# A hybrid attention and state-space layer on one core: loads moved from SyncE's queue to GpSimd's, context products issued a quarter unit behind the latent ones, and one PSUM bank for the state updates of both directions

## The chip, the core and the metric

One core of a Trainium2 chip (trn2) runs the kernel as a single program. The engines are TensorE (PE; its weight loads are listed apart as PEld), VectorE (DVE), ScalarE (ACT), GpSimd (POOL) and SyncE (SP). DMAs can be issued from a queue of SP, ACT or POOL. The metric is the device time of one execution in microseconds (us); lower is better.

## The reference, cut to what matters

One layer (`D_MODEL` 2048) of a diffusion backbone for 512 latent tokens and 256 context tokens, in fp32. A vector `c` gives shift, scale and gate through `w_mod`; the tokens are RMS-normalised, modulated, and multiplied by one wide matrix `w_in`. Its columns feed two groups: windowed attention, and a bidirectional state-space scan (SSD) with four groups `g` of four heads. Both are gated, normalised and put through one output projection.

```python
shift, scale, gate = jnp.split((jax.nn.silu(c) @ w_mod + b_mod)[:, None, :], 3, axis=-1)
px = (rmsnorm(x, norm_g) * (1 + scale) + shift) @ w_in
pc = (rmsnorm(ctx, norm_g) * (1 + scale_c) + shift_c) @ w_in
...
a_cs = jnp.cumsum(a_t, axis=-1)
wts = cb[:, :, None] * jnp.exp(segsum(a_t))
y_diag = jnp.einsum('bgrcls,bcsgrp->bclgrp', wts, xdt)
states = jnp.einsum('bclgn,bgrcl,bclgrp->bcgrpn', bc, decay_states, xdt)
...
y_off = jnp.einsum('bclgn,bcgrpn,bgrcl->bclgrp', cc, prev, jnp.exp(a_cs))
...
x = x + gate * merge_groups(att_x, gx, y_x, zx, att_norm_g, ssd_norm_g, w_out)
```

The scan runs over chunks of 128 tokens, forwards and backwards; the latent scan starts from the state that the context tokens leave.

## The kernel before, in words

The program is written in one function, `emit`, with helpers. It goes through these stages: loading and normalising the latent tokens with the modulation (to some 140 us), the projections of values and step sizes (to 185 us), the SSD stage (unit 0 ends near 197 us; four groups to some 546 us), attention (to some 870 us), and the output projection.

**Units.** A unit is 128 columns of `w_in`. `load_unit` (L307 on) loads it in two halves `wr` of 512 KB from SP's queue, splits each quarter (four of the 16 K tiles of 128 rows) into a high part `wh` (ACT, L317) and a low part `wl` (DVE, by the helper at L55), and hands out (k, wh, wl) tile by tile. `proj` (L325 on) issues for each k three matmuls into `pj` (bank `a`, 128x512, latent tokens) and, for units that context tokens need, three into `pjc` (bank `b`, 128x256). All matmuls go through the helper at L49. The PSUM has eight banks, in pools "mm" (3), "sa" (2), "tp" (2), "pv" (1); `pj` and `pjc` come from "mm".

**A group of the SSD stage** (`ssd_group`, L485 on) has four units: two of `xs`, one of `bT`, each with context, and one of `cT` without. `conv_silu` (L470 on) runs the three-tap convolution of each: ACT at L476, DVE at L477 and L479, on the latent and the context half, then SiLU at L109 and L110; L479 is the last reader of the banks. Then come transposes, the states (`stc` from the context, `stx` in three steps per direction, each a matmul of 128x256 into a "tp" bank, and on DVE a product with the decay `etot` and an addition of the bank into `stt`), and for each of two pairs of heads: `z` (off-diagonal part), rows of running sums loaded from a DRAM scratch `csd` and spread over partitions (`ec`, two loads of 128 KB each, L570; `df`, 256 KB, L581), the decay matrices on ACT (L584 to L588) and DVE, and `yps`.

**Gate steps.** The modulation's gate (2048 columns) is summed on DVE: 64 steps `gate_step` (L280 on), called four times in each of units 1 to 16, each adding one 128x512 tile of `w_mod` times a scalar into `ga` (L299). The tiles `wg` are loaded two steps ahead into two buffers (L297); the tie `issue_after` puts each on SP's queue behind the unit's `wr` load. At each of four column blocks `ga` is cleared by a POOL memset (L289), gets its bias row (L291), and its sum over partitions is a matmul `gp`, stored to `grow`.

**What sets the order.** A planner orders each engine's instructions at build time, by their place in the source, by priorities (`tc.high_priority`: 200 for weights and the convolution, 150 for `df` and `ec` loads) and by costs of its own; it places an instruction where it expects its inputs to be there. It also puts in the waits. On the chip each engine and each DMA queue keeps that order: what waits at the head of a queue holds back what is behind it.

Of the kernel before, what the change touches and what calls it, by code (L numbers as in the profile page):

```python
# [14 lines left out]
P = 128  # L15
D = 2048
KT = 16
# [26 lines left out]
def emit(tc, xin, ctxT, wmod, wgate, bgate, wz, wvd, wu, wo, fng, vecs, cst, rope, out, dbg=None):  # L44
    nc = tc.nc
    es = ExitStack()

    def mm(o, l, r, start, stop):
        return nc.tensor.matmul(o, l, r, start=start, stop=stop)  # L49
# [13 lines left out]
    with es:  # L63
# [5 lines left out]
        def bank(tag, name, dt=F32, shape=(P, 512)):  # L69
            return ps.tile(list(shape), dt, tag=tag, name=name, bufs=pcount[tag])  # L70
# [23 lines left out]
        xl, cl = [], []  # L94
# [121 lines left out]
        for j in range(KT):  # L216
            mt = bank("pv", f"md_{j}", shape=(P, 260))
            md, ms = mt[:, 0:256], mt[:, 256:260]
            for hf in range(4):
                wm = su.tile([P, 4, 256], F32, tag="wm", name=f"wm_{j}_{hf}", bufs=7)  # L220
                nc.sync.dma_start(wm, wmod[j, :, hf * 4:hf * 4 + 4, :])
                for ki in range(4):
                    k = hf * 4 + ki
# [56 lines left out]
        def gate_step(ld):  # L280

            i = next(gsteps, None)
            if i is None:
                return
            n, k = divmod(i, KT)
            if k == 0:
                ga = wp.tile([P, 512], F32, tag="ga", name=f"ga_{n}", bufs=1)
                gacc.append(ga)
                nc.gpsimd.memset(ga, 0.0)  # L289
                with tc.issue_after(ld.ins):  # L290
                    nc.sync.dma_start(ga[0:1, :], bgate[:, n * 512:(n + 1) * 512])  # L291
            ga = gacc[n]
            for ii in range(len(gw), min(i + 2, 4 * KT)):
                n_, k_ = divmod(ii, KT)
                gw.append(gbuf(ii % 2, f"wg_{n_}_{k_}"))
                with tc.issue_after(ld.ins):
                    nc.sync.dma_start(gw[ii], wgate[n_, k_])  # L297
            wg = gw[i]
            geng.scalar_tensor_tensor(out=ga, in0=wg, scalar=sc0[:, k:k + 1], in1=ga, op0=ALU.mult, op1=ALU.add)  # L299
            if k == KT - 1:  # L300
                gp = bank("tp", f"gp_{n}", shape=(1, 512))
                mm(gp, ones[:, 0:1], ga, True, True)
                nc.scalar.activation(ga[0:1, :], gp, AF.Copy)
                nc.sync.dma_start(grow[:, n * 512:(n + 1) * 512], ga[0:1, :])
# [20 lines left out]
        def proj(u, with_ctx):  # L325
            a = bank("mm", f"pj_{u}")
            b = bank("mm", f"pjc_{u}", shape=(P, CT)) if with_ctx else None
            for k, wh, wl in load_unit(u):
                s0, s1 = k == 0, k == KT - 1
                mm(a, wh, xh[k], s0, False)  # L330
                mm(a, wh, xl[k], False, False)
                mm(a, wl, xh[k], False, s1)
                if with_ctx:
                    mm(b, wh, ch[k], s0, False)
                    mm(b, wh, cl[k], False, False)
                    mm(b, wl, ch[k], False, s1)
            return a, b


# [145 lines left out]
        def ssd_group(g, units):  # L485
# [41 lines left out]
            for d in range(2):  # L527
# [3 lines left out]
                mm(sp_, btok[:, 5, :], xw(d, 5), False, True)  # L531
                nc.scalar.activation(stt_[d][:, first, :], sp_, AF.Copy)
            for stp in range(3):
                for d in range(2):
                    c = stp if d == 0 else 3 - stp
                    nx = c + 1 if d == 0 else c - 1
                    sp_ = bank("tp", f"stx_{g}_{d}_{c}", shape=(P, 256))
                    mm(sp_, btok[:, c, :], xw(d, c), True, True)
                    tt(nc.vector, stt_[d][:, nx, :].rearrange("p (a b) -> p a b", a=4),
                       stt_[d][:, c, :].rearrange("p (a b) -> p a b", a=4),  # L540
                       etot[:, d, c, hs].unsqueeze(2).to_broadcast([P, 4, HD]), ALU.mult)
                    tt(nc.vector, stt_[d][:, nx, :], stt_[d][:, nx, :], sp_, ALU.add)
# [12 lines left out]
            for pr in range(2):  # L555
                tix = 2 * g + pr

                zs = []
                for d in range(2):
                    z = bank("sa", f"z_{tix}_{d}")  # L560
                    for c in range(NT):
                        cc = slice(c * P, (c + 1) * P)
                        mm(z[:, cc], stt_[d][:, c, pr * P:(pr + 1) * P], cT[:, cc], True, True)
                    zs.append(z)
                ecs = [w2(f"ec_{tix}_{d}", "ec", 3) for d in range(2)]

                for d in range(2):
                    with tc.high_priority(HB):
                        for hh in range(2):
                            nc.sync.dma_start(ecs[d][hh * 64:hh * 64 + 64], csd[d * 16 + tix * 2 + hh].partition_broadcast(64))  # L570
                    nc.scalar.activation(ecs[d], ecs[d], AF.Exp)
                yps = bank("pv", f"yps_{tix}")
                dm = []
                for hh in range(2):
                    r = tix * 2 + hh
                    dx = []
                    for d in range(2):

                        df = w2(f"df_{r}_{d}", "df", DF)
                        with tc.high_priority(HB):  # L580
                            nc.sync.dma_start(df, csd[d * 16 + r].partition_broadcast(P))  # L581
                        for c in range(NT):
                            cc = slice(c * P, (c + 1) * P)
                            nc.scalar.activation(df[:, cc], df[:, cc], AF.Relu, bias=cs[:, d, c, r:r + 1], scale=-1.0)  # L584
                        nc.scalar.activation(df, df, AF.Exp, scale=-1.0)
                        for c in range(NT):
                            cc = slice(c * P, (c + 1) * P)
                            nc.scalar.activation(df[:, cc], df[:, cc], AF.Copy, scale=dtt[:, d, c, r:r + 1])  # L588
                        tt(nc.vector, df, df, cb[d], ALU.mult)
                        dx.append(df)  # L590
                    tt(nc.vector, dx[0], dx[0], dx[1], ALU.add)
                    dm.append(dx[0])

                for c in range(NT):
                    cc = slice(c * P, (c + 1) * P)
                    for hh in (1, 0):
                        hl = pr * 2 + hh
                        mmo(yps[hh * 64:hh * 64 + 64, cc], xtok[:, c, hl * HD:hl * HD + HD], dm[hh][:, cc], True, True)
                for d in range(2):
                    tt(nc.vector, ecs[d], zs[d], ecs[d], ALU.mult)  # L600
                tt(nc.vector, ecs[0], ecs[0], ecs[1], ALU.add)
                yt = w2(f"yt_{tix}", "cve", 1)
                nc.vector.scalar_tensor_tensor(out=yt, in0=xs[pr][:, 0:S], scalar=dskh[:, tix:tix + 1], in1=yps,
                                               op0=ALU.mult, op1=ALU.add)
                tt(nc.vector, yt, yt, ecs[0], ALU.add)
                tt(nc.vector, yT[tix], yT[tix], yt, ALU.mult)
# [415 lines left out]
```

## Time and profile before

| | |
|---|---|
| median of three runs | 1055.41 us (1053.86 to 1055.51) |
| the profiled execution, its span | 1056.66 us, 1054.8 us |
| PE, PEld busy | 1011.6 us (96%), 818.4 us (78%) |
| DVE, ACT, POOL busy | 690.2 us (65%), 535.9 us (51%), 141.2 us (13%) |
| DMA | 147.29 MB in 53403 packets, 42.0% of 16 engines, all program loads on SP's queue |

Matmuls overlap: a 128x512 matmul shows 0.40 us, while the next begins 0.23 us later. So the busy share of PE says where it stands idle, and start-to-start times say what a product costs. "Idle before" of an engine is put down to what ended it. The granted clock of PE is 1.00 at its full 2.4 GHz and 0.5 at 1.2 GHz.

### The profile page before, as it was taken

Reading aid. Unit: us, or ns where it says so; the run is one execution under the profiler, and the core shown is the slowest. Engines: PE = TensorE matmul, PEld = TensorE weight load, DVE = VectorE, ACT = ScalarE, POOL = GpSimd, SP = SyncE. Lnnn points to the kernel's source line nnn. Section 1 sums busy time; section 2 is a strip of 40 time slices with the busy share of each in tenths; the row PEclk is TensorE's granted clock in tenths of the full one; section 3 lists DMA queues with packets and bytes.
Section 4 is the critical chain, followed back from the end, with each engine's and each line's share of the span. In section 5 each row is a group of like instructions: output and inputs, shape, how many; then the busy total and the mean of one; then the engine's idle time right before and its main releaser. Section 6 shows DMA issues by size and latency. Waiting matters only on the chain.

```text
span 1054.8 us, 15544 instructions
## 1 busy us (share of the span) xinstructions
PE 1011.6 (96%) x5682; PEld 818.4 (78%) x5682; DVE 690.2 (65%) x1346; ACT 535.9 (51%) x1236; POOL 141.2 (13%) x96
## 2 busy tenths in 40 slices
PE   5999999999999998999999999999999998999996
PEld 4676789887877887778787778777777777888885
DVE  4323378454875875785778888788797865333765
ACT  6222265247385384285364567576666654333333
POOL 0232300000000000000007000000000018644220
PEclk8999999999999999999999999999999998999999
DMA  9999963263273273264131311112111135442304
GB/s 332 382 340 351 340 219 120 92 214 121 78 232 122 80 219 113 89 203 127 61 106 61 100 41 61 41 40 81 40 58 59 45 135 195 141 167 90 106 27 159
DMA packets 53403, 147.29 MB, mean 140 GB/s; under 512 B 6056, under 2 KB 6568, under 8 KB 53072
## 3 DMA queue, kind: packets, MB, share of 16 engines
q1 hardware_dynamic: 53328, 146.31, 42.0%
q8 instruction: 44, 0.72, 0.3%
q14 instruction: 31, 0.25, 0.1%
HBM read 142.02 MB, written 4.27 MB: 139 GB/s over the span
## 4 chain that ended last, share of the span: by engine, by line
PE 58%; DVE 11%; DMA 9%; ACT 5%; issue 2%; POOL 1%; SPq 0%; ACTq 0%; DVEq 0%; POOLq 0%
PE pj L49 26%; PE o L49 14%; DMA wg<-in_wgate_dram 4%; PE pjc L49 4%; PE pv L49 3%; DMA ec<-csd 3%; PE ptp L768 3%; PE sl L49 3%; DVE df L55 2%; DVE wl L55 2%; PE sc L49 2%; DVE ga L299 1%; PE stx L49 1%; PE stc L49 1%; ACT df L588 1%
## 5 line engine op out<-in xcount | busy, mean ns | idle before, releaser
L49 PE MATMUL pj<-xh,wl 128*128 128x512 f32 x560 | 224.4, 401 | 1.5 <-DVE wl L55 1.4
L49 PE MATMUL pj<-xh,wh 128*128 128x512 f32 x560 | 225.8, 403 | 0.0
L49 PE MATMUL pj<-xl,wh 128*128 128x512 f32 x560 | 224.2, 400 | 0.0
L317 ACT ACTIVATE wh<-wr 128x512 fp32r<-128x512 f32 x140 | 87.6, 629 | 138.2 <-PE pjc L49 67.6
L55 DVE TENSOR_TENSOR wl<-wr,wh 128x512 fp32r<-128x512 f32 x140 | 100.1, 718 | 62.7 <-ACT wh L317 55.3
L49 PEld LDWEIGHTS pj<-xh,wl 128*128 128x128 f32 x560 | 105.8, 189 | 22.8 <-DVE wl L55 2.4
L49 PEld LDWEIGHTS pj<-xh,wh 128*128 128x128 f32 x560 | 106.2, 190 | 16.8 <-ACT wh L317 3.5
L49 PEld LDWEIGHTS pj<-xl,wh 128*128 128x128 f32 x560 | 106.3, 190 | 13.4
L55 DVE TENSOR_TENSOR wol<-wo,woh 128x512 fp32r<-128x512 f32 x56 | 54.4, 985 | 65.2 <-ACT woh L858 58.9
L49 PE MATMUL pjc<-chq,wh 128*128 128x256 f32 x224 | 66.5, 297 | 11.3 <-DVE xs L479 11.3
L858 ACT ACTIVATE woh<-wo 128x512 fp32r<-128x512 f32 x56 | 34.8, 629 | 73.4 <-PE o L49 65.3
L299 DVE SCALAR_TENSOR_TENSOR ga<-wg,sc,ga 128x512 f32<-128x512 f32 x64 | 47.9, 748 | 34.4 <-DMA wg<-in_wgate_dram 34.4
L49 PE MATMUL pjc<-clq,wh 128*128 128x256 f32 x224 | 65.6, 293 | 0.0
L49 PE MATMUL pjc<-chq,wl 128*128 128x256 f32 x224 | 63.8, 285 | 0.0
L49 PEld LDWEIGHTS pjc<-chq,wh 128*128 128x128 f32 x224 | 42.9, 191 | 22.3 <-ACT wh L317 14.2
L55 POOL TENSOR_TENSOR hacc<-hacc,hsq 128x512 f32<-128x512 f32 x14 | 20.4, 1457 | 290.0 <-ACT hsq L666 286.6
L772 ACT ACTIVATE ph<-ptp 128x512 fp32r<-128x512 f32 x72 | 41.1, 597 | 28.2 <-PE ptp L768 26.7
L49 PE MATMUL o<-woh,hsh 128*128 128x512 f32 x128 | 52.0, 407 | 3.1 <-ACT part L877 3.1
L55 DVE TENSOR_TENSOR pl<-ptp,ph 128x512 fp32r<-128x512 f32 x72 | 48.5, 684 | 7.9 <-ACT ph L772 7.7
L743 ACT ACTIVATE pe<-sl,nm 128x256 f32<-128x256 f32 (+1 forms) x64 | 33.6, 525 | 35.7 <-DVE nm L741 34.0
L49 PE MATMUL o<-wol,hsh 128*128 128x512 f32 x128 | 51.2, 400 | 0.0
L49 PE MATMUL o<-woh,hsl 128*128 128x512 f32 x128 | 51.1, 399 | 0.0
(282 smaller groups left out, 2294.0 us busy)
## 6 DMA issues: line engine op xcount, KB each, us to landing
wr<-in_wu_dram SPq DMA_DIRECT2D x70, 512.0 KB, 3.7
wm<-in_wmod_dram SPq DMA_DIRECT2D x64, 512.0 KB, 8.7
wg<-in_wgate_dram SPq DMA_DIRECT2D x64, 256.0 KB, 3.4
wo<-in_wo_dram SPq DMA_DIRECT2D x32, 512.0 KB, 3.9
df<-csd SPq DMA_DIRECT2D x32, 256.0 KB, 3.9
wsr<-in_wz_dram SPq DMA_DIRECT2D x16, 448.0 KB, 5.9
wr_v<-in_wvd_dram SPq DMA_DIRECT2D x16, 288.0 KB, 3.4
xt<-in_xin_dram SPq DMA_DIRECT2D x8, 512.0 KB, 4.7
```

Of the source, the lines that this page charges most:

```text
L49: return nc.tensor.matmul(o, l, r, start=start, stop=stop)
L55: eng.tensor_tensor(out=o, in0=a, in1=b, op=op)
L299: geng.scalar_tensor_tensor(out=ga, in0=wg, scalar=sc0[:, k:k + 1], in1=ga, op0=ALU.mult, op1=ALU.add)
L317: nc.scalar.activation(wh, rr, AF.Copy)
L588: nc.scalar.activation(df[:, cc], df[:, cc], AF.Copy, scale=dtt[:, d, c, r:r + 1])
L743: nc.scalar.activation(pe[:, 0:nl * P], sl, AF.Exp, bias=nm[:, i:i + 1], accum_out=sm[:, i, 0:1])
L768: nc.tensor.transpose(tp[:, i * P:(i + 1) * P], pt[i][:, n * P:(n + 1) * P], ident)
L772: nc.scalar.activation(ph, tp, AF.Copy)
L858: nc.scalar.activation(wh, wr[:, i, :], AF.Copy)
```

## The change

It has three parts. Gate weights `wg`, and the rows of running sums `ec` and `df`, are issued from POOL's queue instead of SP's, the gate weights without the tie to the `wr` load. In `proj` the context products of four K tiles are issued together after the latent products of these four. In the state updates both directions of a step write two halves of one "tp" bank instead of a bank each. Nothing else is changed, and the same sums are computed.

```diff
@@ gate_step
             for ii in range(len(gw), min(i + 2, 4 * KT)):
                 n_, k_ = divmod(ii, KT)
                 gw.append(gbuf(ii % 2, f"wg_{n_}_{k_}"))
-                with tc.issue_after(ld.ins):
-                    nc.sync.dma_start(gw[ii], wgate[n_, k_])
+                nc.gpsimd.dma_start(gw[ii], wgate[n_, k_])
@@ proj
             b = bank("mm", f"pjc_{u}", shape=(P, CT)) if with_ctx else None
+            late = []
             for k, wh, wl in load_unit(u):
                 s0, s1 = k == 0, k == KT - 1
                 mm(a, wh, xh[k], s0, False)
                 mm(a, wh, xl[k], False, False)
                 mm(a, wl, xh[k], False, s1)
                 if with_ctx:
-                    mm(b, wh, ch[k], s0, False)
-                    mm(b, wh, cl[k], False, False)
-                    mm(b, wl, ch[k], False, s1)
+                    late.append((k, wh, wl))
+                    if k % 4 == 3:
+                        for kk, h, l in late:
+                            mm(b, h, ch[kk], kk == 0, False)
+                            mm(b, h, cl[kk], False, False)
+                            mm(b, l, ch[kk], False, kk == KT - 1)
+                        late = []
@@ ssd_group
             for stp in range(3):
+                sp2 = bank("tp", f"stx_{g}_{stp}", shape=(P, 2, 256))
                 for d in range(2):
                     c = stp if d == 0 else 3 - stp
                     nx = c + 1 if d == 0 else c - 1
-                    sp_ = bank("tp", f"stx_{g}_{d}_{c}", shape=(P, 256))
+                    sp_ = sp2[:, d, :]
                     mm(sp_, btok[:, c, :], xw(d, c), True, True)
...
-                            nc.sync.dma_start(ecs[d][hh * 64:hh * 64 + 64], csd[d * 16 + tix * 2 + hh].partition_broadcast(64))
+                            nc.gpsimd.dma_start(ecs[d][hh * 64:hh * 64 + 64], csd[d * 16 + tix * 2 + hh].partition_broadcast(64))
...
-                            nc.sync.dma_start(df, csd[d * 16 + r].partition_broadcast(P))
+                            nc.gpsimd.dma_start(df, csd[d * 16 + r].partition_broadcast(P))
```

## Rows read from the trace of the kernel before

**Rows 1.** Busy time by stretch, the SSD stage: start:end, length, then busy us (instructions) by engine.
```profile
197.00:546.00 349.00, 333.74 (x1911) 279.80 (x1910) 237.25 (x419) 190.33 (x456) 1.58 (x3) 0.99 0.45 137
```
**Rows 2.** Waits of PE: engine, line, what for; total us, times, longest.
```profile
PE pjc L49 <- DVE xs L479: 11.3, 7, 3.2
```
**Rows 3.** Timeline of PE: start us, us, instruction, and idle time before it.
```profile
394.97 0.28 PE L49 MATMUL pjc<-chq,wh 128*128 128x256 f32 x1
...
395.33 0.39 PE L49 MATMUL pj<-xh,wh 128*128 128x512 f32 x1
...
397.89 0.40 PE L49 MATMUL pj<-xh,wl 128*128 128x512 f32 x1
401.52 0.35 PE L49 MATMUL pjc<-chq,wh 128*128 128x256 f32 x1 [3.24 <-DVE xs L479]
...
319.73 0.36 PE L49 MATMUL pjc<-chq,wh 128*128 128x256 f32 x1 [0.74 <-DVE xs L479]
...
380.70 0.36 PE L49 MATMUL pjc<-chq,wh 128*128 128x256 f32 x1 [0.84 <-DVE xs L479]
```
**Rows 4.** Busy time by stretch, 2 us each; the granted clock stands after POOL's count.
```profile
240.00:242.00 2.00, 2.00 (x16) 1.88 (x15) 1.36 (x2) 2.00 (x6) 0.00 (x0) 1.00 0.14 37
...
402.00:404.00 2.00, 2.00 (x11) 2.00 (x11) 1.99 (x3) 1.48 (x4) 0.00 (x0) 0.51 0.18 53
404.00:406.00 2.00, 2.00 (x8) 1.66 (x8) 1.36 (x2) 1.94 (x5) 0.00 (x0) 0.64 0.92 303
```
**Rows 5.** Timeline of DVE ahead of the wait at 401.52.
```profile
397.23 0.75 DVE L299 SCALAR_TENSOR_TENSOR ga<-wg,sc,ga 128x512 f32<-128x512 f32 x1 [3.19 <-DMA wg<-in_wgate_dram]
...
400.25 0.47 DVE L477 SCALAR_TENSOR_TENSOR xs<-pjc,v_sb,xs 128x255 f32<-128x255 f32 x1
400.64 0.74 DVE L479 SCALAR_TENSOR_TENSOR xs<-pj,v_sb,xs 128x511 f32<-128x511 f32 x1
```
**Rows 6.** Waits of DVE and ACT from 197 to 560 us.
```profile
DVE ga L299 <- DMA wg<-in_wgate_dram: 31.9, 24, 3.2
...
ACT df L584 <- DMA df<-csd: 15.0, 13, 3.4
...
ACT ec L571 <- DMA ec<-csd: 9.6, 7, 2.6
```
**Rows 7.** Waits of SP's queue from 197 to 560 us.
```profile
SPq L312 <- DVE wl L55: 121.6, 31, 10.1
SPq L297 <- DVE ga L299: 64.1, 43, 7.0
```
**Rows 8.** Timeline of SP's queue, two loads in a row.
```profile
392.21 0.33 SPq L297 DMA_DIRECT2D wg<-in_wgate_dram  x1
392.58 0.45 SPq L570 DMA_DIRECT2D ec<-csd  x1
```
**Rows 9.** Loads: count, KB, median us to landing; issue ns min/median/max, first and last start.
```profile
wg<-in_wgate_dram SPq DMA_DIRECT2D x64, 256.0 KB, 3.4
...
df<-csd SPq DMA_DIRECT2D x32, 256.0 KB, 3.9
...
ec<-csd SPq DMA_DIRECT2D x32, 128.0 KB, 5.6
...
L297 SPq DMA_DIRECT2D wg<-in_wgate_dram x64: 327/328/710, 157.1 to 485.5; - x64
```
**Rows 10.** POOL: a group of the page (busy us, mean ns, idle before), and its timeline.
```profile
L55 POOL TENSOR_TENSOR hacc<-hacc,hsq 128x512 f32<-128x512 f32 x14 | 20.4, 1457 | 290.0 <-ACT hsq L666 286.6
...
265.20 0.53 POOL L289 MEMSET ga<- 128x512 f32 x1 [127.75 <-DMA grow<-ga]
```
**Rows 11.** Timeline of SP's queue, the next two gate loads.
```profile
271.30 1.43 SPq L297 DMA_DIRECT2D wg<-in_wgate_dram  x2
```
**Rows 12.** State updates: matmul (ns min/median/max, first and last start), and two additions on DVE's timeline.
```profile
L49 PE MATMUL stx<-xw,btok x48: 377/379/483, 273.4 to 522.4; 128*128 128x256 f32 x48
...
274.38 0.94 DVE L55 TENSOR_TENSOR stt<-stt,stx 128x256 f32<-128x256 f32 x2
```

## The prediction, made before the changed kernel was run

> **What bounds it now.** I read first the busy time by stretches, then who waits for whom on TensorE (PE), then single boundaries in the timeline. The change touches only the SSD stage, 197 to 546 us: there PE is busy for 333.74 of 349 us [rows 1], so without new idle time elsewhere all that can be won is some 15 us of idle time and what a lowered clock costs. Of that idle time 11.3 us stand in seven waits of one kind: the first context product `pjc` of a projection unit waits for VectorE's (DVE's) L479 of the unit before [rows 2]. The reason is the PSUM pool: three "mm" banks, so the new `pjc` gets the bank of the old `pj`, and that is free when the convolution has read it.
>
> The reader should look at one such place [rows 3]. The new unit's `pj` begins at 395.33 and twelve of its products are issued up to 397.89; then PE stands for 3.24 us until L479 is done. So the planner already puts twelve latent products ahead of the first context product, and they don't suffice. The waits at 319.73 (0.74) and 380.70 (0.84) are the shortest of the seven; the other five are 1.57 us or more each. The 3.24 us cost more than themselves: behind them the granted clock is 0.51 and 0.64 for 2 us each, between the levels of 1.2 and 2.4 GHz [rows 4], which loses 2 x 0.49 + 2 x 0.36 = 1.7 us.
>
> Why is L479 late? On DVE a gate step waits 3.19 us for its weights, and the convolution is behind it [rows 5]. Over the stage DVE waits 31.9 us in 24 places for gate weights, and ScalarE (ACT) 15.0 and 9.6 us for the rows of running sums `df` and `ec` [rows 6]. The loads themselves wait at the head of SyncE's (SP's) one queue: 64.1 us for a gate buffer that DVE still reads, 121.6 us for a `wr` buffer [rows 7]. At 392.21 a gate load goes out, and the `ec` load behind it only at 392.58 [rows 8].
>
> **The context products.** Number and length stay. In the interleaved order three context products take 395.33 - 394.97 = 0.36 us, so 0.12 each [rows 3]. The last latent product of a unit is followed by three of them before and by twelve after, so `pj` is whole 9 x 0.12 = 1.08 us earlier against the unit's end, and the planner, which knows this, can put the convolution of `pj` that much further ahead of gate steps and `df` work on DVE and ACT. Each of the seven waits can shrink by that, but not below nothing: 5 x 1.08 + 0.74 + 0.84 = 7.0 us. With 3.24 cut to 2.2 I expect no fall of the clock behind it, as it stays at 1.00 behind the wait of the same kind that ends at 239.7 [rows 4]: 1.7 us more. Bounds: nothing, if the backlog and not the end of `pj` sets the convolution's start; and 8.9 us, if L479 of `pj` also overtakes the `pjc` half of L477 that now stands between (0.39 us from 400.25 to 400.64 [rows 5], 5 x 1.47 + 1.58). The `wh` and `wl` buffers stay in use to the end of the same quarter, so nothing new waits there.
>
> **The other queue.** SP loses 64 gate loads at 0.33 us of issue and 32 each of `df` and `ec` [rows 9]; it keeps the `wr` loads, and since no row of the stage has ACT waiting for `wr`, that alone is worth nothing. GpSimd (POOL) gets all 128. They still stand in one queue: a gate load that waits for DVE holds the `df` and `ec` behind it as before; only the waits for `wr` are taken out. Three memsets of `ga` are in that queue too; the first runs at 265.20 [rows 10] and the next gate load went out at 271.30 [rows 11], so it holds nothing back. The trace has no load issued from POOL. From below: no dearer than SP's 0.33 us. From above: POOL's two-input work on 128x512, 1.46 us; its memset of the same tile takes 0.53 [rows 10]. I take 0.53, as writing without reading is nearest to issuing, so 0.2 us more per load. Gate loads take 3.4 us to land [rows 9], and two buffers make the steps wait for them, so each of the 24 waits grows by 0.2: 4.8 us on DVE. About half of this reaches PE, as much of DVE's waiting falls where PE has work: +2.4 us. Against that stands that the `wr` waits no longer hold up loads; rows 7 show them, but not a load that was late by them, so I count nothing. The Trainium skill (DMA: Bandwidth & Descriptors, section "Latency and other measured facts") gives some 1 us to the first byte from GpSimd's queue against 0.6 us from SP's; no run here shows it. By that the term would be about 4.8 us instead of 2.4, an estimate.
>
> **The state updates.** Three steps in four groups take one bank instead of two. The matmul is 0.38 us, and the two additions now run as a pair, 0.94 us from 274.38 [rows 12]. No wait of PE or DVE for them is in the rows, so nothing is to be won; they lie between `pj` products. Taken at 0; the bounds stand with the rival below.
>
> **The sum.** The profiled execution took 1056.66 us (its span 1054.8 and 1.86 around it), 1.25 over the median of the runs. 1056.66 - 7.0 - 1.7 + 2.4 = 1050.4, so 1049.1 against the median of 1055.41. A measurement here can tell some 0.2% (2 us) from no change.
>
> **Rivals.**
> - **POOL issues dearly (slower).** At 1.46 us each of the 24 waits grows by 1.13: 27.1 us on DVE, half of it on PE 13.6. Less 8.7 from the context products that is +4.9: 1060.3; if all of it got through, 1073.8. It turns slower where 12 x (price - 0.33) passes 8.7, so at 1.05 us per load. For it: 128 loads in one in-order queue, in bursts of four `ec`. Against: POOL is idle in this stage but for memsets. 0.27.
> - **The deferral does nothing.** The planner already has twelve products ahead of the wait, and if DVE's backlog sets L479, the order that is written out changes nothing: 1055.4 + 2.4 = 1057.8. 0.15, half of it within 0.2%.
> - **The shared bank makes PE wait.** If the second direction's matmul may not write the bank while DVE adds the first, each of twelve pairs is a round trip: one addition (0.42) and a handover (L479's end at 401.38 to 401.52, 0.14), 0.56 x 12 = 6.7 us at worst, if PE stands meanwhile: 1049.1 + 6.7 = 1055.8. The rows speak half against it: other products lie between, which the planner can use. 0.07. The Trainium skill (PSUM — Partial Sum Buffer, section "PSUM bank collisions raise a hardware error") states that two engines must not touch one bank at once even at different addresses, so such a wait has to be there; no row here has such a pair.
> - **The planner sorts it all out.** With other costs for POOL's loads it may put gate steps where their data is there, and the convolutions first: then all of the 11.3 and the clock's 1.7 go, 13.0 us: 1042.4. For it: real loads came later than the order of DVE's steps assumed, 24 times. 0.15.
>
> **How the numbers follow.** My forecast, 1049.1, has 0.36. Faster is that and the last rival, 0.51; slower the first rival and half of the second, 0.34; within 0.2% the other half and the shared bank, 0.15. The forecast's own range is 1044 to 1055 (8.9 won and no dearer queue, or nothing but the clock's 1.7). Since both signs hold much, the range goes down to 1040 for the last rival and up to 1064, past 1060.3 part of the way to 1073.8.
>
> **What would show it.** Right: the seven waits of `pjc` for `xs` L479 sum to 3 to 5 us; runs of twelve `pjc` all through a unit; on DVE both halves of the `pj` convolution adjacent; no 0.5 clock near 403; waits for gate weights around 37 us. Wrong: these waits at 11 us or more (the queue, if gate waits grew with them; the backlog, if they didn't); new waits of PE's `stx` for DVE's `stt` (the bank); `ec` or `df` landing over 2 us later than 5.6 and 3.9 (POOL's issue). If gate waits shrink well under 30 us, the planner has moved the steps.

## The result, and the profile after

The kernel after takes 1064.63 us (median of 4 executions, 1063.37 to 1065.74) against 1054.89 us for the kernel before in the same sessions (1053.86 to 1055.51). The ratio is 1.0109, with a 95% interval of 1.0081 to 1.0138; the two medians alone make 1.0092, 9.7 us. The profiled execution of after took 1063.37 us, its span 1061.5. So the change costs some 10 to 11 us, where a gain to 1049.1 was forecast. The time lies inside the range, and on the other side of the sign.

Busy time by stretch of after: start:end, length, busy us (instructions) of PE, PEld, DVE, ACT and POOL, granted clock, DMA share, GB/s. The first row answers to [rows 1], the other three are three groups of the SSD stage.
```profile
197.00:546.00 349.00, 330.28 (x1880) 276.83 (x1879) 234.63 (x414) 185.46 (x447) 69.19 (x129) 0.99 0.45 135
262.00:345.00 83.00, 76.92 (x441) 64.27 (x440) 56.96 (x98) 45.70 (x111) 17.17 (x32) 0.98 0.48 140
345.00:427.00 82.00, 77.81 (x446) 65.34 (x444) 56.50 (x98) 45.26 (x110) 17.69 (x33) 0.98 0.47 140
427.00:507.00 80.00, 74.20 (x431) 62.81 (x431) 55.30 (x97) 44.62 (x109) 16.62 (x31) 0.98 0.46 133
```
The same view of before, for the two stretches where its clock was below 1.00:
```profile
190.00:262.00 72.00, 68.42 (x363) 58.24 (x361) 39.11 (x72) 35.73 (x80) 0.00 (x0) 0.98 0.49 150
...
345.00:427.00 82.00, 77.69 (x444) 65.08 (x443) 56.94 (x98) 45.79 (x111) 0.53 (x1) 0.98 0.47 141
```
In the same 349 us PE is busy 3.5 us less, so idle time grew. The clock lost about 245 x 0.02 = 4.9 us in after, 154 x 0.02 = 3.1 us in before (rounded to 0.01, so to some 2 us).

Who waits for whom in after, 197 to 560 us: engine, line, what for; total us, times, longest. These answer to [rows 2, 6].
```profile
PE pjc L49 <- DVE xs L484: 9.3, 4, 3.1
PE pjc L49 <- ACT wh L316: 7.2, 3, 3.0
PE yps L49 <- DVE df L55: 3.5, 2, 2.7
...
DVE ga L298 <- DMA wg<-in_wgate_dram: 33.3, 29, 3.7
...
ACT df L590 <- DMA df<-csd: 17.5, 13, 3.0
ACT ec L577 <- DMA ec<-csd: 9.7, 6, 3.2
...
POOL wg L296 <- DVE ga L298: 88.6, 47, 5.9
```
(Lines have moved: the convolution is L482 and L484, the gate step L298, its load L296, the split of the weights on ACT L316.) The waits of `pjc` are 16.5 us instead of 11.3, and 7.2 of them are new: they wait for ACT, not for the convolution. Two places show how. First the timeline of PE and of DVE at the worst of the four:
```profile
318.99 0.35 PE L49 MATMUL pjc<-chq,wh 128*128 128x256 f32 x1 [3.14 <-DVE xs L484]
...
320.62 0.41 PE L49 MATMUL pjc<-chq,wl 128*128 128x256 f32 x1
320.83 0.63 PE L49 MATMUL pj<-xh,wh 128*128 128x512 f32 x1
```
```profile
314.96 0.74 DVE L482 SCALAR_TENSOR_TENSOR xs<-pj,v_sb,xs 128x511 f32<-128x511 f32 x1
317.43 0.75 DVE L298 SCALAR_TENSOR_TENSOR ga<-wg,sc,ga 128x512 f32<-128x512 f32 x1 [1.73 <-DMA wg<-in_wgate_dram]
318.10 0.74 DVE L484 SCALAR_TENSOR_TENSOR xs<-pj,v_sb,xs 128x511 f32<-128x511 f32 x1
```
The planner did bring the convolution of `pj` forward, but put a gate step between its two halves, and that waits for its load. PE stands for 3.14 us, and then a product of 0.40 us takes 0.63: the clock is down, its granted share being 0.51 from 320 to 322 us. The waits at 403.56 and 488.30, of 2.1 and 2.8 us, are the same place in the next two groups. Then the timeline of ACT and PE:
```profile
291.99 0.63 ACT L577 ACTIVATE ec<-ec 128x512 f32<-128x512 f32 x1 [2.31 <-DMA ec<-csd]
...
295.98 0.62 ACT L316 ACTIVATE wh<-wr 128x512 fp32r<-128x512 f32 x1
```
```profile
296.65 0.36 PE L49 MATMUL pjc<-chq,wh 128*128 128x256 f32 x1 [2.17 <-ACT wh L316]
```
A row that lands late holds ACT, and the next quarter's `wh` behind it is late for PE. This too comes again in the next two groups.

The loads of after (count, KB, median us to landing; then the gate load's issue in ns, min/median/max) answer to [rows 9]:
```profile
wg<-in_wgate_dram POOLq DMA_DIRECT2D x64, 256.0 KB, 3.5
df<-csd POOLq DMA_DIRECT2D x32, 256.0 KB, 4.1
ec<-csd POOLq DMA_DIRECT2D x32, 128.0 KB, 5.1
...
L296 POOL DMA_DIRECT2D wg<-in_wgate_dram x64: 538/538/715, 137.1 to 490.5; - x64
```
Nothing in them is far from before: an issue of 0.54 us, landings within 0.5 us of [rows 9]. What cost 10 to 11 us had to be found by parts.

### The profile page after: what moved, and what is told of

The parts are those of the page before. It is cut to its first block, busy times and chain, and to the rows that moved or that the text cites. A ratio compares the mean times of both kernels' runs of the same rounds, so it can differ in the third digit from the quotient of the medians.

```text
span 1061.5 us, 15568 instructions
## 1 busy us (share of the span) xinstructions
PE 1012.6 (95%) x5682; PEld 819.3 (77%) x5682; DVE 692.1 (65%) x1346; ACT 536.5 (51%) x1236; POOL 209.5 (20%) x224
## 4 chain that ended last, share of the span: by engine, by line
PE 73%; DMA 8%; DVE 6%; ACT 6%; issue 4%; POOL 2%; SPq 0%; ACTq 0%; POOLq 0%; DVEq 0%
PE pj L49 25%; PE o L49 14%; PE zps L49 7%; DMA wg<-in_wgate_dram 5%; PE vps L49 4%; PE md L49 3%; PE pv L49 3%; PE pjc L49 3%; PE ptp L774 3%; PE sl L49 3%; DMA ec<-csd 2%; PE sc L49 2%; PE stx L49 1%; DVE df L55 1%; ACT df L594 1%
## 5 line engine op out<-in xcount | busy, mean ns | idle before, releaser
L316 ACT ACTIVATE wh<-wr 128x512 fp32r<-128x512 f32 x140 | 87.6, 628 | 140.2 <-PE pjc L49 68.9
L49 PE MATMUL pjc<-chq,wh 128*128 128x256 f32 x224 | 65.0, 290 | 16.5 <-DVE xs L484 9.3
L298 DVE SCALAR_TENSOR_TENSOR ga<-wg,sc,ga 128x512 f32<-128x512 f32 x64 | 47.9, 748 | 33.3 <-DMA wg<-in_wgate_dram 33.3
L296 POOL DMA_DIRECT2D wg<-in_wgate_dram x64 | 35.0, 547 | 171.8 <-DVE ga L298 88.6
L55 POOL TENSOR_TENSOR wsl<-wsr,wsh 128x896 fp32r<-128x896 f32 x16 | 33.9, 2118 | 101.4 <-ACT wsh L231 101.4
```

The lines of the kernel that those rows point to most:

```text
L55: eng.tensor_tensor(out=o, in0=a, in1=b, op=op)
L296: nc.gpsimd.dma_start(gw[ii], wgate[n_, k_])
L316: nc.scalar.activation(wh, rr, AF.Copy)
```

## The experiments

All times below are medians beside runs of before on the same chip; ratios are to before with their 95% interval. "Stage" is the time from the first product into `cst_ps` to the first of the last `yps`, read from PE's timeline of the one profiled execution (before 215.72 to 544.52, after 212.99 to 550.47). "`pjc` waits" is all that PE waits before `pjc` products there. The table names each kernel by its text of expectation. That execution need not be the median one: before's took 1056.66 us, and those of `wa` and `ra`, 1069.41 and 1081.1, are 5 us over their medians. So differences of stages hold to some 5 us.

| kernel | gate loads, rows, weights on | us | ratio | stage us | `pjc` waits us |
|---|---|---|---|---|---|
| before | SP, SP, SP | 1052 to 1055 | 1 | 328.8 | 11.3 |
| after | POOL, POOL, SP | 1064.63 | 1.0109 (1.0081 to 1.0138) | 337.5 | 16.5 |
| `a_only`: deferral alone | SP, SP, SP | 1047.65 | 0.9962 (0.994 to 0.9983) | 321.5 | 5.3 |
| `c_only`: shared bank alone | SP, SP, SP | 1048.28 | 0.9951 (0.9928 to 0.9973) | 324.4 | 10.6 |
| `ac`: both | SP, SP, SP | 1047.21 | 0.9953 (0.9932 to 0.9974) | 321.4 | 5.4 |
| `st`: no tie | SP, SP, SP | 1048.32 | 0.9972 (0.9951 to 0.9993) | 322.6 | 8.3 |
| `b_only`: queue alone | POOL, POOL, SP | 1076.32 | 1.0223 (1.0181 to 1.0264) | 351.4 | 23.5 |
| `bw` | POOL, SP, SP | 1064.58 | 1.0102 (1.0066 to 1.0139) | 340.3 | 19.4 |
| `br` | SP, POOL, SP | 1071.13 | 1.0169 (1.0132 to 1.0205) | 346.0 | 22.6 |
| `pool_stage` | POOL, POOL, POOL | 1061.23 | 1.0094 (1.0064 to 1.0124) | 333.6 | 15.8 |
| `full_stage`: after, so | POOL, POOL, POOL | 1056.71 | 1.0052 (1.003 to 1.0074) | 329.9 | 10.1 |
| `wa` | SP, SP, ACT | 1064.44 | 1.0108 (1.0066 to 1.0151) | 346.1 | 23.9 |
| `ra` | SP, ACT, SP | 1076.02 | 1.0227 (1.0172 to 1.0281) | 350.0 | 25.5 |

**1. Which of the three parts?** Each part alone, and the deferral with the bank. `a_only` has the hunk of `proj` alone, `c_only` that of the state updates, `b_only` the three hunks with `nc.gpsimd`, `ac` the first two of these:
```diff
 # b_only
-                with tc.issue_after(ld.ins):
-                    nc.sync.dma_start(gw[ii], wgate[n_, k_])
+                nc.gpsimd.dma_start(gw[ii], wgate[n_, k_])
...
-                            nc.sync.dma_start(df, csd[d * 16 + r].partition_broadcast(P))
+                            nc.gpsimd.dma_start(df, csd[d * 16 + r].partition_broadcast(P))
```
Expected, for the deferral alone:

> Only the context products are deferred; the loads stay on SyncE's queue and the state updates keep a bank each. Theory Q (the queue: loads issued from GpSimd's queue make the gate and row waits longer, and the loss of 9.7 us is theirs): this kernel gains what the prediction gave it, 1045 to 1051 us. Theory D (the deferral: the planner now takes the convolution apart, with gate steps and their waits between its two halves, and the bank comes free later): this kernel carries the loss, 1060 to 1066 us. Theory S (the shared bank): within 2 us of before.

For the queue alone:

> Only the loads of gate weights and of the rows of running sums go to GpSimd's queue. Theory Q: 1060 to 1068 us, with the waits of VectorE for gate weights and of ScalarE for rows longer than before (31.9, and 15.0 and 9.6 us). Theory D: within 3 us of before, 1052 to 1058 us. Theory S: within 2 us of before.

For the bank alone:

> Only the state updates of both directions share a bank. Theory S: 1058 us or more, with new waits of TensorE or VectorE in the state updates. Theories Q and D: within 3 us of before.

For the deferral and the bank:

> Context products deferred and the shared bank, loads left on SyncE's queue: the change without its queue part. Theory Q: 1045 to 1052 us. Theory D: 1060 to 1066 us, as the changed kernel. If the parts act on one another through the order that the planner makes, it lies neither at the sum of the two kernels with one part each nor at one of these values.

Measured: the queue alone costs 2.2%, some 23 us, more than the 1060 to 1068 us expected; deferral, bank and both together each gain 0.4 to 0.5%, and for the bank nothing was expected. So the loss is the queue's, all of it. With deferral and bank it costs 1.0109 - 0.9953 = 1.6%, some 16 us. The two profiled spans say where: after 1061.5, `ac` 1045.5, 16.0 us apart. PE's waits at `pjc` and `yps` are 20.0 us in after and 5.4 + 3.2 = 8.6 in `ac`, 11.4 more; the clock, 1.00 in every stretch of `ac`, lost 4.9 us in after: 16.3 together. PE's waits with `a_only`, then `ac`, as in [rows 2]:
```profile
PE pjc L49 <- DVE xs L484: 5.3, 6, 1.2
```
```profile
PE pjc L49 <- DVE xs L484: 5.4, 6, 1.2
```
What a long wait costs beyond itself shows in `b_only`, PE's timeline:
```profile
326.25 0.36 PE L49 MATMUL pjc<-chq,wh 128*128 128x256 f32 x1 [4.21 <-DVE xs L478]
...
326.96 0.41 PE L49 MATMUL pjc<-clq,wh 128*128 128x256 f32 x1
327.17 0.41 PE L49 MATMUL pjc<-chq,wl 128*128 128x256 f32 x1
```
Products that begin 0.12 us apart at full clock begin 0.21 apart here, and the granted clock is 0.50 from 328 to 330 us. In `b_only` the clock was 0.95, 0.98, 0.94 and 0.94 over 72, 83, 82 and 80 us, 15 us lost against 3.1 in before; the waits grew by 12.2. The sum, 24, is the stage's growth of 22.6 to within the rounding.

**2. Gate loads, rows, or the lost tie?** DVE's written order of gate steps and convolutions is before's in `bw` and `st` from the second group on, and in `b_only` but for a few places in each group. The cleanest is `bw` against `st`: in the stage one of PE's 1900 instructions, two of DVE's and some 17 of ACT's 450 stand elsewhere. So DVE's written order is not what costs there. `bw` and `br` have one half of the queue's edit each; `st` drops the tie and leaves everything on SP:
```diff
 # st
-                with tc.issue_after(ld.ins):
-                    nc.sync.dma_start(gw[ii], wgate[n_, k_])
+                nc.sync.dma_start(gw[ii], wgate[n_, k_])
```
Expected of the gate loads alone:

> Before, with the 64 gate loads alone on GpSimd's queue and not tied to the weight loads; the row loads stay on SP. VectorE's written order is that of before from the first group on. Theory T1 (two gate buffers go round more slowly: each issue takes 0.54 us instead of 0.33 and is released later, so bursts of gate steps end later and the convolution behind them too): most of the queue's cost is here, ratio 1.010 to 1.022, TensorE's waits of pjc for the convolution 18 us or more against 11.3. Rival T2 (in one in-order queue row loads stand behind gate loads that wait for a free buffer, which ScalarE then waits for; it takes both kinds of loads on GpSimd's queue): within 0.4% of before. Rival T3 (the row loads alone are what comes late): within 0.4%. Rival T4 (the tie to the weight loads was what mattered): as T1 here, and the same in the kernel that only drops the tie.

Of the rows alone:

> Before, with the 64 row loads alone (ec and df) on GpSimd's queue; gate loads stay on SP and tied. T1: within 0.4% of before. T2: within 0.4%, or a little faster, since nothing that waits for the gate steps stands ahead of the rows. T3: ratio 1.012 to 1.022, with ScalarE's waits for df and ec clearly over the 24.6 us of before.

Of the tie:

> Before, with the gate loads on SP's queue as before but not tied to the weight load. VectorE's written order is that of before from the first group on. T4 (the tie mattered): ratio 1.010 or more, as with the gate loads alone on GpSimd's queue. T1, T2, T3: within 0.3% of before.

Measured: the tie is worth nothing (without it the kernel is 0.3% faster, so `bw`, which drops it too, costs 1.3% against `st`). Each half costs by itself, 1.0% and 1.7%, and the two together cost less than their sum. T1 got the size of the gate loads but expected nothing of the rows, T2 expected nothing of either half, so both fell; T3 got the size of the rows right and missed the gate loads. What the rows do in `br` can be read from POOL's queue and from DVE behind it:
```profile
217.29 1.72 POOL L570 DMA_DIRECT2D ec<-csd  x3 [79.43 <-DVE xs L477]
219.00 0.57 POOL L581 DMA_DIRECT2D df<-csd  x1
219.56 0.53 POOL L570 DMA_DIRECT2D ec<-csd  x1
220.08 1.65 POOL L581 DMA_DIRECT2D df<-csd  x3
221.72 1.05 POOL L570 DMA_DIRECT2D ec<-csd  x2
223.10 0.57 POOL L581 DMA_DIRECT2D df<-csd  x1 [0.33 <-issue]
```
```profile
226.90 0.75 DVE L299 SCALAR_TENSOR_TENSOR ga<-wg,sc,ga 128x512 f32<-128x512 f32 x1 [5.26 <-DMA wg<-in_wgate_dram]
232.35 0.75 DVE L299 SCALAR_TENSOR_TENSOR ga<-wg,sc,ga 128x512 f32<-128x512 f32 x1 [4.70 <-DMA wg<-in_wgate_dram]
...
238.58 1.54 DVE L299 SCALAR_TENSOR_TENSOR ga<-wg,sc,ga 128x512 f32<-128x512 f32 x2 [3.54 <-DMA wg<-in_wgate_dram]
```
Eleven rows go out one behind the other in 6.4 us, as their buffers are free. In before they stood in SP's queue with gate loads between them, and each gate load's wait for its buffer held them back. The gate steps now wait up to 5.26 us for loads on SP's queue that nobody touched (3.2 at most in [rows 6]), the convolution is behind them, and PE's longest wait there is 6.7 us. The rows themselves come late too: ACT waits 32.3 us for them, against 24.6 in [rows 6].

**3. The split of one queue, or GpSimd's queue?** That suggests that not GpSimd's queue but having two queues is what costs. `all_pool` puts the weights of all units and the gate's four bias rows on GpSimd's queue too, with the tie, so that one queue holds everything in nearly the order of before's SP queue; `full_all` does it to the kernel after; `hb400` stays on SP and only groups the rows by a higher priority.
```diff
 # all_pool, on top of b_only
-                    ld = nc.sync.dma_start(wr, wu[u, :, hf * 8:hf * 8 + 8, :])
+                    ld = nc.gpsimd.dma_start(wr, wu[u, :, hf * 8:hf * 8 + 8, :])
...
+                with tc.issue_after(ld.ins):
+                    nc.gpsimd.dma_start(gw[ii], wgate[n_, k_])
 # hb400
-DF, HB = 5, 150
+DF, HB = 5, 400
```


> Before, with every load of these units on GpSimd's queue: gate weights (tied to the weight load again), rows of running sums, and the projection weights too. So there is one in-order queue again, and the order written into it is nearly that of before's SP queue, with a gate load between the rows. Theory P (what costs is that with two queues the order between gate loads, rows and weights is lost: whatever has a free buffer goes out at once, rows in bursts, and the gate loads that the convolution stands behind land late): within 0.5% of before, TensorE's waits of pjc 9 to 14 us. Rival L (loads from GpSimd's queue are slower each, by their issue of 0.54 us or their handling): ratio 1.020 or more, since 36 weight loads more go the slow way, waits of pjc over 22 us.

> The kernel after, with the projection weights on GpSimd's queue too and the gate loads tied to them again, so that one in-order queue holds all loads. P: the time of deferral and shared bank with all loads on SP, ratio 0.993 to 1.000. L: ratio 1.012 or more, over that of the kernel after (1.0109).

> Before, all loads on SP, with the planner's priority of the row loads raised from 150 to 400, which groups the rows ahead of the gate loads in SP's queue (five rows in a row where there was a gate load between). P: the rows go out in bursts here too: ratio 1.004 to 1.015, VectorE's longest wait for a gate load over 4 us against 3.2. L: within 0.4% of before, as nothing goes through GpSimd's queue.

Measured: `all_pool` 1068.46 us, ratio 1.0163 (1.0111 to 1.0215), `pjc` waits 16.9 us: between the two theories. `full_all` 1063.16, 1.0118 (1.007 to 1.0166), no better than after and close to theory L's 1.012. But the stage tells another story than the whole: 336.0 us in `all_pool` against 351.4 in `b_only`, and 327.2 in `full_all` against 337.5 in after. What was won there was lost elsewhere, as weights of earlier and later units had moved too: `full_all` is 5.4 us later than `ac` at the first `cst_ps` and takes 5.4 us more behind the last `yps`. And `hb400` came out faster, 1046.44, 0.9935 (0.9914 to 0.9955), where theory P wanted it slower: rows in a burst do no harm in one queue. DVE's written order differs there, so it says no more than that.

So the weights of the sixteen units with gate steps alone (with the tie and the bias rows) went to GpSimd's queue, in before (`pool_stage`) and in after (`full_stage`):
```diff
 # pool_stage, full_stage
-                    ld = nc.gpsimd.dma_start(wr, wu[u, :, hf * 8:hf * 8 + 8, :])
+                    ld = (nc.gpsimd if 1 <= u < 17 else nc.sync).dma_start(wr, wu[u, :, hf * 8:hf * 8 + 8, :])
```


> Before, with all loads of the sixteen units that carry gate steps in GpSimd's queue (gate loads tied, rows, and these units' weights); weights of all other units stay on SP. If the split of one queue is the larger part: from the first cst product to the last yps 333 to 338 us (before 328.8, the split kernel 351.4) and ratio 1.004 to 1.010. If GpSimd's queue itself is the larger part: 345 us or more and ratio 1.016 or more.

> The kernel after, with the weights of the sixteen units that carry gate steps on GpSimd's queue too and the gate loads tied, the other weights on SP. If the split is the larger part: first cst product to last yps 325 to 330 us (after 337.5, deferral and bank on SP alone 321.4), ratio 0.998 to 1.004. If GpSimd's queue itself is: 335 us or more, ratio 1.010 or more.

Measured: ratio 1.0094 and a stage of 333.6 us, 1.0052 and 329.9 us. More loads on GpSimd's queue make the kernel faster, as long as all that compete are in it: against the split kernels 1.3% (`b_only`, some 14 us) and 0.6% (after, some 6 us). In `b_only` and `pool_stage` DVE's written order is the same ahead of the convolutions but for one gate step in a group; in `full_stage`, from the second group on, no gate step stands between the halves of a convolution as it does in after, so the 6 us hold that difference too. What stays is 0.9% over before and 1.0% over `ac`, some 10 us in both. I put it down to GpSimd's queue itself; no kernel here takes it apart from what the planner moved along with it (some 25 of ACT's 450 instructions of the stage stand elsewhere in either). `full_stage` came out 0.1% over the range expected for it.

The other half of the argument is a split without GpSimd. `wa` puts the weights of the sixteen units on ScalarE's queue and drops the tie, `ra` puts the rows there:
```diff
 # wa
-                    ld = nc.sync.dma_start(wr, wu[u, :, hf * 8:hf * 8 + 8, :])
+                    ld = (nc.scalar if 1 <= u < 17 else nc.sync).dma_start(wr, wu[u, :, hf * 8:hf * 8 + 8, :])
```


> Before, with the weights of the sixteen units that carry gate steps issued from ScalarE's queue; gate loads (not tied) and rows keep their places in SP's queue. If a split of the one queue costs by itself (6 to 14 us by the runs so far): ratio 1.005 to 1.015, some gate loads landing after 6 us or more (before 4.9 at most). If only GpSimd's queue costs: ratio 0.994 to 1.002. ScalarE issues 32 loads more; at SP's 0.33 us each that is some 10 us of an engine that is not the bound.

> Before, with the 64 row loads issued from ScalarE's queue in its own stream of work; weights and gate loads stay on SP. If a split costs by itself: ratio 1.005 to 1.017 (the rows on GpSimd's queue: 1.0169). If only GpSimd's queue costs: 0.994 to 1.003; 64 issues at 0.39 us are 25 us more on ScalarE, which also waits for the rows, so a part of that may show.

Measured: 1.0108 (1.4% against `st`, which drops the tie as well) and 1.0227, above the range expected, without one load of this stage on GpSimd's queue. In `wa` the rows and gate loads stay on SP, and before the convolutions DVE's order of gate steps is that of `b_only` but for one step in the first group. It is not a clean split, though: the planner moved some 130 of PE's 1900 instructions of the stage against `st`, 50 of DVE's 417 and 70 of ACT's 450. Two rows, from SP's queue and DVE's timeline, show a gate load that is issued at 228.58 and lets its step begin at 236.18, 7.6 us later (the step at 227.80 freed this buffer, and with two buffers the step at 236.18 is the one that reads it next):
```profile
228.58 0.49 SPq L296 DMA_DIRECT2D wg<-in_wgate_dram  x1
```
```profile
236.18 0.75 DVE L298 SCALAR_TENSOR_TENSOR ga<-wg,sc,ga 128x512 f32<-128x512 f32 x1 [5.29 <-DMA wg<-in_wgate_dram]
```
Its longest landing is 8.0 us, against 4.9 in before and 5.6 in `st`. `ra` is no cleaner, as 64 issues on ACT are some 25 us of work on an engine that PE waits for.

Why two queues are worse than one is only partly shown. In `br` the rows above point to the burst. In `wa` most weight loads go out as their buffer comes free, as before, and some gate loads still land late: five take over 6.5 us from issue to the step that stands waiting for them, where the longest of before and `st` take 5.7 and 5.5. All five were issued 1 to 3 us behind a weight load, as the one at 228.58 was behind that of 227.47. The trace counts packets by queue; in `wa`, from 230.5 to 231.5 us, ACT's queue (q10) and SP's (q1), packets, MB and share of the 16 DMA engines:
```profile
q10 hardware_dynamic: 55, 0.22, 78.5%
q1 hardware_dynamic: 23, 0.03, 19.9%
```
So in this 1 us ACT's queue had four fifths of the DMA engines' time, while loads of SP's queue were under way. The Trainium skill (DMA: Bandwidth & Descriptors, section "Queues, rings and completion order") states that each DMA engine goes round the queues that have work, a packet at a time. The trace agrees in so far as the two queues overlap; on which engine a packet ran it doesn't tell. In one queue a weight load ahead would hold up a gate load too, so why it lands later with two is not shown. Nor do late gate loads explain all: `hb400` and `ac_st`, each on one queue and faster than before, have two over 6.5 us, and after has none (5.5 at most). So in after the loss is not in such late gate loads; a gate step between the halves of a convolution and rows that land late on ACT are what its trace shows.

**4. What GpSimd's queue itself costs.** A gate load that waits for its buffer starts when the step before has ended. In before the step of 308.14 ends at 308.89 and SP's load starts at 308.93; in `b_only` the step of 314.65 ends at 315.40 and POOL's starts at 315.69:
```profile
308.14 0.75 DVE L299 SCALAR_TENSOR_TENSOR ga<-wg,sc,ga 128x512 f32<-128x512 f32 x1 [0.17 <-DMA wg<-in_wgate_dram]
```
```profile
308.93 0.33 SPq L297 DMA_DIRECT2D wg<-in_wgate_dram  x1
```
```profile
314.65 0.75 DVE L298 SCALAR_TENSOR_TENSOR ga<-wg,sc,ga 128x512 f32<-128x512 f32 x1 [3.06 <-DMA wg<-in_wgate_dram]
```
```profile
315.69 0.57 POOL L296 DMA_DIRECT2D wg<-in_wgate_dram  x1 [3.33 <-DMA wg<-in_wgate_dram]
```
Of the 62 gate loads that take over a buffer, 55 start 0.03 us after the step in before; 58 of `b_only` and 61 of after start 0.29 to 0.30 after it. With the issue, 0.54 for 0.33, a load leaves by this reckoning 0.27 + 0.21 = 0.48 us later. For the 24 places of [rows 6] where DVE waits for one this makes 11.5 us. But the two kernels with one queue on GpSimd don't show so much: DVE waits for gate loads 38.4 us in `pool_stage`, 6.5 more than in before, and 33.3 in `full_stage`, 5.8 more than the 27.5 of `ac`. So by way of the gate loads the price covers some 6 of the 10 us at most; what comes by way of the rows and weights, or of the order, is open. Work of DVE that holds up POOL's issues is not it: of the 64 gate loads of after none took over 0.72 us to issue.

**5. Gate steps off DVE.** `ac_gp` takes the deferral and the bank and moves the gate steps to GpSimd, to see whether they are what holds the convolution:
```diff
-        geng = nc.vector
+        geng = nc.gpsimd
...
-            geng.scalar_tensor_tensor(out=ga, in0=wg, scalar=sc0[:, k:k + 1], in1=ga, op0=ALU.mult, op1=ALU.add)
+            geng.tensor_scalar(out=wg, in0=wg, scalar1=sc0[:, k:k + 1], scalar2=None, op0=ALU.mult)
+            tt(geng, ga, ga, wg, ALU.add)
```


> The deferral and the shared bank with every load on SP as before, and the gate steps moved from VectorE to GpSimd as a product and a sum each (twice as many instructions). If what TensorE still waits for at pjc is the gate steps that stand before the convolution on VectorE: these waits fall from 5.4 us to under 2 us and the time to 1041 to 1046 us. If it is the convolution's own length and ScalarE's part of it: 1046 to 1048 us with the waits near 5 us. If GpSimd slows VectorE by sharing its way to SBUF: VectorE's tensor_tensor rows grow from 0.69 us and the time is over 1050 us.

Measured: 1082.24, ratio 1.0287 (1.0246 to 1.0329). The third case held in time and in part of the rows: some of DVE's own work grew, though the median did not. A group of DVE in `ac`, then in `ac_gp` (ns min/median/max, first and last start):
```profile
L55 DVE TENSOR_TENSOR df<-df,cb x32: 682/687/695, 278.4 to 534.2; 128x512 f32<-128x512 f32 x32
```
```profile
L55 DVE TENSOR_TENSOR df<-df,cb x32: 675/692/1811, 290.0 to 570.4; 128x512 f32<-128x512 f32 x32
```
Single ones take 1.8 us instead of 0.69. Of DVE's 48 products of `df` in this stage 15 took over 0.9 us, and each of these ran while POOL was computing; of the other 33, 20 ran with POOL idle. Whether the gate steps are what holds the convolution can't be read from it, since DVE's other work became slower at the same time.

**6. A version that beats both.** `ac` beats before and after. Two more were tried, without the tie (`ac_st`), and with the rows' priority at 400 (`ac_hb400`, the edit of `hb400` on `ac`).

> Deferral and shared bank, all loads on SP, the gate loads no longer tied to the weight load. If the small gains of each edit alone (0.3 to 0.5%) come from different waits, they add: ratio 0.989 to 0.993. If each of them only moves before's one long wait of 3.24 us and its half clock out of the way: ratio 0.994 to 0.997, as with any one of them.

> Deferral and shared bank, all loads on SP, with the planner's priority of the row loads at 400 in place of 150. If the gain of the priority (0.9935) adds to that of deferral and bank (0.9953): ratio 0.987 to 0.991. If all of them take away the same few waits: 0.993 to 0.996.

Measured: `ac_st` 1046.85, 0.9941 (0.9913 to 0.997): nothing over `ac`. `ac_hb400` 1043.76, 0.9924 (0.9899 to 0.995), between its two expected ranges, `pjc` waits 4.2 us, stage 320.4: the lowest median, and its interval overlaps that of `ac`, so whether the priority adds to it stays open.

## Why the prediction was wrong

- **The step that failed is the queue's term**, +2.4 us, where the runs show some +16 (after against `ac`). It had two halves. "They still stand in one queue" was true of the 128 loads, but the loads that they compete with, the weights, were left on the other, and for the loss of that order I counted "nothing". It costs some 14 us alone (`b_only` against `pool_stage`), and in the whole change up to 6 (after against `full_stage`), with a gate step inside the convolution in this figure. The other half is the price of a load: I took 0.2 us more (0.53, and 0.54 was measured for the issue), but the start is late by 0.27 as well, so 0.48. "About half of this reaches PE" can't be checked as it stands: with all loads on GpSimd's queue some 10 us are lost, while DVE's gate waits grow by only some 6. So why the second half is as large as it is stays open.
- **The sum of DVE's gate waits was the wrong gauge.** The signs said "gate waits around 37 us". They were 33.3 in after, 34.9 in `b_only`, 31.9 before: hardly longer, while PE's waits rose from 11.3 to 16.5 and 23.5. What counts is which wait stands ahead of a convolution, not how long all are.
- **The deferral was right** in sign and in what it does to the waits, but not in size. The seven waits fell to 5.3 us in six places (3 to 5 expected), the longest from 3.24 to 1.2, and the clock stayed at 1.00 throughout. 8.7 us were forecast, and 0.4% (0.2 to 0.6%) came, some 4 us. The stage of `a_only` is 7.4 us shorter, but against the one profiled execution of before, a long one for this kernel, from which the 8.7 were read too. And `c_only`, where these waits stay at 10.6 us, gains as much; so how much of the 4 us is due to the waits is not shown. In after its gain is still there but buried: the runs of twelve `pjc` go through each unit, but the halves of the convolution are not adjacent, since from the second group on a gate step went between the latent ones.
- **The shared bank did no harm.** After has no wait of PE before `stx`, and the 48 products take 0.38 us as in [rows 12]. Whether it gains is not shown: `c_only` is 0.5% faster, but `st`, which changes nothing that PE does, gains 0.3%, and the gains don't add (`ac` 0.9953). The state updates themselves changed little: in `c_only`, from the `gp` of a group to its first `yps`, it takes 24.24 us for 24.57 in the first group, about the same in the next two, and 23.48 for 23.23 in the last. What all these kernels share is that the one wait of 3.24 us [rows 3] and the clock's fall behind it [rows 4] are gone; that this is the whole of it was argued, not tried.
- **The rivals.** "POOL issues dearly" had the right sign and, at 1060.3, nearly the right time, for the wrong reason: an issue costs 0.54 us, not 1.46, and its turning point of 1.05 us per load was never reached. "The deferral does nothing" and "the shared bank makes PE wait" fell. So did "the planner sorts it all out": it put gate steps in front of convolutions as before, and in after between their halves. The page of the Trainium skill named beside the queue's term (DMA: Bandwidth & Descriptors, section "Latency and other measured facts"), some 0.4 us more to the first byte, comes near the 0.48 measured for start and issue, though that is not the same stretch; by it the term was 4.8 us, an estimate, still a third of what came.

## What to carry to other kernels

A DMA queue in which everything waits behind everything is also a schedule: before moving loads out of it, ask what order it kept, and move the loads that compete together or not at all (here `pool_stage` lost 0.9% where `b_only` lost 2.2%). Price a moved load by its whole round, from the release of its buffer to its start, issue and landing, and look for it where an engine's in-order stream has something urgent right behind the wait; a total of waits hides it. And when a change has several parts, run each alone early: two of the three here were gains that the third covered.

## What was not expected of the hardware

- A load on GpSimd's queue starts 0.30 us after the work that releases it, on SP's 0.03 us.
- A kernel whose loads are split between SP's and ScalarE's queues, `wa`, is as slow as one with the gate loads moved to GpSimd's (1.0108 and 1.0102), with other changes of order in it.
- GpSimd's product and sum on 128x512 tiles (1.82 and 1.36 us mean) stretched single two-input operations of DVE from 0.69 to 1.81 us.
- The kernel before varies by 1% from one execution to the next, and its time goes with the granted clock: of 86 executions, ten at a mean clock of 0.988 took 1055.8 us on average (1054.1 to 1058.5), six at 0.994 took 1049.2. The profiled one [rows 1 to 4] was one at 0.988, so its 3.24 us wait and half clock need not be there each time.
